# A float32 kernel of mixers, attention and FFNs: small steps of its stages rebuilt and reordered

## The chip, the core and the metric

The kernel runs on one core of a Trainium2 chip. The metric is device time in microseconds of one execution, and the time of a kernel is the median over its runs. One execution was also recorded by the hardware profiler; its rows are quoted below. TensorE is called PE, its weight loads PEld, VectorE DVE, ScalarE ACT, GpSimd POOL, and the engine that issues most of the transfers SP.

## The reference, cut to what matters

Two blocks run over 256 tokens of width 1024, all in float32. The first has two layers, each of four sublayers; the second has one layer.

```python
for l in range(2):
    h = swiglu(rms_norm(x, norm_pre[l, 0]), ffn1_gate[l], ffn1_up[l], ffn1_down[l])
    x = x + 0.5 * rms_norm(h, norm_post[l, 0])
    h = parallel_head_groups(rms_norm(x, norm_pre[l, 1]), ...)      # retention and gated delta rule
    x = x + rms_norm(h, norm_post[l, 1])
    h = memory_cross_attention(rms_norm(x, norm_pre[l, 2]), rms_norm(mem, mem_norm[l]), ...)
    ...
```

In `parallel_head_groups` the gated delta rule works on four heads, two directions and chunks of 64 tokens. It needs the decays, which are exponentials of differences of running sums of `g` within a chunk, and the solution of a unit lower triangular system per chunk:

```python
g = jnp.cumsum(g.reshape(b, h, n, c), axis=-1)
decay = jnp.exp(jnp.where(tril, g[..., :, None] - g[..., None, :], -jnp.inf))
lower = jnp.where(strict, jnp.einsum('bhnid,bhnjd->bhnij', k_beta, k) * decay, 0.0)
sol = lax.linalg.triangular_solve(lower, rhs, left_side=True, lower=True, unit_diagonal=True)
```

## The kernel before

**Tiling.** The 256 tokens are two tiles of 128 (`t` = 0, 1). Stages follow one another: `ffn1_0`, `mix_0`, `xat_0`, `ffn2_0`, the same four with `_1`, then the second block (`blk2_0`: a mixer, and a last `ffn`). Every large product is three products of split operands: `mm3` (L168) multiplies high by high, high by low and low by high part, each in one pass. A weight unit comes by SP into one of four `raw` buffers, and `unit` (L135) makes its high part on ACT (L148) and its low part on DVE (L149), in the pools `wts` (4 buffers, `self.wp`) or `w2` (8 buffers). Products that are not split run in plain float32; the trace shows each of those as two matmul records, and the transposes as one.

**Order.** The program is traced in order, and a planner sets each engine's queue: by the order of the program, except that an instruction whose operands are late in the planner's own estimate lets later ones pass. An engine then runs its queue strictly in order. `tc.issue_after(ins)` puts what a block traces on the engine of `ins` behind it.

**Stage ends.** `residual` (L286) takes a stage's sums from PSUM, norms them (`rstd`, L208: squares on ACT, then eight instructions on one column, L213 and L189 to L193, on POOL), scales them (`hg`, L296, L298) and adds them to `x` (L300). `set_pre` (L254) then prepares the next stage's input: `xg` is `x` times the gain (L235), or also times another `rstd` where the norm isn't deferred (L237). `take_pre` transposes `xg` on PE (L250) and splits it into `xT`. The end of tile 1 is kept in `self.late` and run by `run_late` inside the next stage.

**FFN** (L312). `by_tokens(t, j)` (L348) is 24 products of 512 columns for one tile and one slice `j` of the hidden width, followed by a tanh on ACT (L364) and `h` on DVE (L365, L366); `flush` transposes `h` (L371). `by_channels` does the slices from 2 on for both tiles at once. `DN(t, j)` (L408), 12 products of 512 columns, adds slice `j` to the output. The entry is L429 to L461: `by_tokens(0, 0)`, `run_late`, `by_tokens(0, 1)` with `take_pre(1)` inside it, and only later `by_tokens(1, 0)` and `(1, 1)`. At the end come `DN(0, 8)` to `DN(0, 10)`, tile 0's residual, and `DN(1, 7)` to `DN(1, 10)`. `wpool` (L329) names the pool of each unit.

**Mixer** (L724). A stream of projections (`fill`) is advanced by `more()` between the steps of the chains. `strengths` makes `g`; `decays` (L795) makes, per direction, three banks of running sums by float32 products (L805), two of them with a mask product (L807), and four exponentials from each. `inverse` (L1024) inverts the triangular blocks per direction: it copies 16 blocks into `md` (L1034, 16 ACT instructions for both directions), transposes them on DVE (L1038), and runs a long elimination on DVE (L1050, L1051). `solve` (L1117) applies the inverse to both directions by products on a quarter of PE each: direction 0 uses one half of the partitions and direction 1 the other (L1145, L1153). `rotary_tables` (L644) is called once by a hook of `ffn1_0`.

**Start.** `build` (L1786 to L1802) runs 16 products on zeros, loads tile 0 of `x`, the gain broadcast to all partitions (512 KB), two weight units, tile 1 of `x` and two more units. The identity that transposes need lies in `cst`, loaded by POOL (L84).

## Time and profile before

| | us |
|---|---|
| median of 3 runs | 1946.12 (1944.95 to 1948.43) |
| profiled execution, its time | 1947.42 |
| its span, first to last instruction | 1945.2 |
| PE busy | 1914.7 (98%) |
| DVE busy | 1412.7 (73%) |
| ACT busy | 1048.9 (54%) |
| POOL busy | 185.7 (10%) |

The span begins and ends 2.2 us inside the execution's own time. The granted clock was 0.998 of full speed over the span. Matmuls are pipelined: an interval between two starts tells what one costs PE, and its own duration is longer than that. A row in brackets names how long the engine sat idle before the instruction and what released it.

### The profile page before, as it was taken

To read this page: it belongs to the slowest core of one execution; us is meant where nothing else is said; L and a number is where in the kernel's file an instruction comes from. 1 tells how busy PE (TensorE), PEld (TensorE's weight loads), DVE (VectorE), ACT (ScalarE), POOL (GpSimd) and SP (SyncE) were. 2 spreads that over 40 slices of the span, in tenths; PEclk is the share of its full clock that TensorE was granted. 3 is DMA by queue.
4 is the path that set the end of the run, shared out by engine and by line. 5 is a ranking of instruction groups with operands and counts; after the bars stand their busy time and mean duration, and the time that the engine had idled before them with its cause. 6 is when DMAs were issued, how large, how long until landed. Compare 5 with 4: busy or idle time off the path is not lost.

```text
span 1945.2 us, 34675 instructions
## 1 busy us (share of the span) xinstructions
PE 1914.7 (98%) x12859; PEld 1717.7 (88%) x12859; DVE 1412.7 (73%) x3002; ACT 1048.9 (54%) x2173; POOL 185.7 (10%) x407
## 2 busy tenths in 40 slices
PE   9999999999999999999999999999999999999998
PEld 6899888898899989999788978998999998888997
DVE  6777688775666766667987757666798988767765
ACT  5655465465554555546555645554555555546542
POOL 2000100020200110010100120002101111001000
PEclk9999999999999999999999999999999999999999
DMA  8666434364566556644434726655566646656651
GB/s 266 206 220 217 125 109 147 109 220 137 164 205 196 180 186 220 187 161 144 137 101 145 247 86 212 200 189 157 146 174 182 187 121 205 200 196 224 199 179 49
DMA packets 272887, 337.26 MB, mean 173 GB/s; under 512 B 19740, under 2 KB 223150, under 8 KB 272718
## 3 DMA queue, kind: packets, MB, share of 16 engines
q1 hardware_dynamic: 266980, 326.64, 53.6%
q10 hardware_dynamic: 5690, 8.25, 1.2%
q8 instruction: 101, 1.65, 0.3%
q14 instruction: 68, 0.56, 0.1%
q0 software_dynamic: 48, 0.16, 0.0%
HBM read 333.90 MB, written 1.08 MB: 172 GB/s over the span
## 4 chain that ended last, share of the span: by engine, by line
PE 84%; DVE 4%; POOL 3%; DMA 2%; ACT 2%; issue 2%; SPq 0%; ACTq 0%; POOLq 0%; DVEq 0%
PE bank L170 25%; PE bank L171 25%; PE bank L172 25%; DVE lo L149 2%; DMA raw<-in_ffn_up_dram 2%; PE bank L250 1%; POOL t L192 1%; POOL vh L213 1%; POOL y L193 1%; ACT hi L148 1%; PE bank L1003 1%; PE bank L1543 1%; ACT md L1034 1%; PE bank L1153 1%; PE bank L1256 1%
## 5 line engine op out<-in xcount | busy, mean ns | idle before, releaser
L148 ACT ACTIVATE hi<-raw 128x512 fp32r<-128x512 f32 (+1 forms) x1190 | 678.7, 615 | 413.6 <-PE bank L172 96.0
L149 DVE TENSOR_TENSOR lo<-raw,hi 128x512 fp32r<-128x512 f32 (+1 forms) x1190 | 764.7, 680 | 187.1 <-ACT hi L148 178.4
L170 PE MATMUL bank<-xh,hi 128*128 128x256 f32 x2080 | 588.8, 283 | 0.0
L171 PE MATMUL bank<-xl,hi 128*128 128x256 f32 x2080 | 585.1, 281 | 0.0
L172 PE MATMUL bank<-xh,lo 128*128 128x256 f32 x2080 | 584.7, 281 | 0.1
L170 PEld LDWEIGHTS bank<-xh,hi 128*128 128x128 f32 x2080 | 394.2, 190 | 4.1
L171 PEld LDWEIGHTS bank<-xl,hi 128*128 128x128 f32 x2080 | 393.9, 189 | 3.5
L172 PEld LDWEIGHTS bank<-xh,lo 128*128 128x128 f32 x2080 | 394.5, 190 | 0.6 <-DVE lo L149 0.6
L170 PE MATMUL bank<-hi,xh 128*128 128x512 f32 (+1 forms) x852 | 333.5, 392 | 3.5 <-ACT xh L175 2.2
L171 PE MATMUL bank<-lo,xh 128*128 128x512 f32 (+1 forms) x852 | 324.7, 381 | 5.2 <-DVE lo L149 5.1
L172 PE MATMUL bank<-hi,xl 128*128 128x512 f32 (+1 forms) x852 | 323.9, 380 | 0.5 <-DVE xl L177 0.5
L171 PEld LDWEIGHTS bank<-lo,xh 128*128 128x128 f32 x852 | 160.3, 188 | 34.8 <-DVE lo L149 9.9
L170 PEld LDWEIGHTS bank<-hi,xh 128*128 128x128 f32 x852 | 160.2, 188 | 31.5 <-ACT xh L175 3.5
L172 PEld LDWEIGHTS bank<-hi,xl 128*128 128x128 f32 x852 | 159.9, 188 | 28.8 <-DVE xl L177 2.2
L170 PE MATMUL bank<-hi,hh 128*128 128x512 f32 x440 | 175.9, 400 | 1.3 <-ACT hh L175 1.3
L171 PE MATMUL bank<-lo,hh 128*128 128x512 f32 x440 | 173.9, 395 | 0.0
L172 PE MATMUL bank<-hi,hl 128*128 128x512 f32 x440 | 173.4, 394 | 0.0
L213 POOL TENSOR_SCALAR vh<-ss 128x1 f32<-128x1 f32 x40 | 27.6, 689 | 1130.8 <-ACT junk L205 996.1
L402 ACT ACTIVATE th<-s 128x256 f32<-128x256 f32 x90 | 37.3, 414 | 124.3 <-DVE s L401 122.7
L172 PEld LDWEIGHTS bank<-hi,hl 128*128 128x128 f32 x440 | 82.7, 188 | 20.7 <-DVE hl L177 0.3
L170 PEld LDWEIGHTS bank<-hi,hh 128*128 128x128 f32 x440 | 82.7, 188 | 18.4 <-ACT hh L175 1.7
L171 PEld LDWEIGHTS bank<-lo,hh 128*128 128x128 f32 x440 | 82.7, 188 | 16.0
(369 smaller groups left out, 1991.4 us busy)
## 6 DMA issues: line engine op xcount, KB each, us to landing
raw<-in_w_in_dram SPq DMA_DIRECT2D x112, 512.0 KB, 4.4
raw<-in_ffn_gate_dram SPq DMA_DIRECT2D x176, 256.0 KB, 3.9
raw<-in_ffn_up_dram SPq DMA_DIRECT2D x176, 256.0 KB, 4.3
raw<-in_ffn_down_dram SPq DMA_DIRECT2D x88, 512.0 KB, 4.6
raw<-in_w_in_dram SPq DMA_DIRECT2D x96, 192.0 KB, 2.8
raw<-in_w_ffn_gate_dram SPq DMA_DIRECT2D x44, 256.0 KB, 3.8
raw<-in_w_ffn_up_dram SPq DMA_DIRECT2D x44, 256.0 KB, 4.1
raw<-in_w_ffn_down_dram SPq DMA_DIRECT2D x22, 512.0 KB, 4.6
```

The source lines that it names most:

```text
L148: nc.scalar.activation(hi[:, c], raw[:, c], AF.Copy)
L149: nc.vector.tensor_tensor(lo[:, c], raw[:, c], hi[:, c].bitcast(F32), ALU.subtract)
L170: mm(out, lhsT=lh, rhs=rh, start=start, stop=False)
L171: mm(out, lhsT=lh, rhs=rl, start=False, stop=False)
L172: mm(out, lhsT=ll, rhs=rh, start=False, stop=stop)
L192: V.tensor_scalar(t, y, y, vh, ALU.mult, ALU.mult)
L193: V.tensor_scalar(y, t, -1.5, y, ALU.add, ALU.mult)
L213: V.tensor_scalar(vh, s[:, 0:1], s[:, 1:2], 0.5 * EPS, ALU.add, ALU.add)
L250: self.nc.tensor.transpose(b[:, i * P:(i + 1) * P], src[:, (q + i) * P:(q + i + 1) * P], self.ident)
L402: last["A"] = nc.scalar.activation(th, s[:, 0], AF.Tanh)
L1003: T.matmul(b[:, j * 256:(j + 1) * 256], lhsT=lhs[:, h, j * P:(j + 1) * P], rhs=rhs[:, h], start=True, stop=True)
L1034: A.activation(md[r, :, :, :, s], mn[r, :, :, c0:c0 + 16].rearrange("p n h a -> p a h n"), AF.Copy, scale=self.half[s][r])
```

## The change

The steps, as they stand in the diff:

- At the start, 12 products on zeros instead of 16; the gain comes as eight rows of 128 (4 KB), is transposed by PE and copied to eight columns; `x` itself is transposed, and the splits of `xT` (one per 128 columns, eight instead of two on ACT and on DVE) multiply by those columns. Tile 1 of `x` is loaded behind one weight unit instead of two.
- In the first stage alone, where `self.late` is None, `by_tokens` of both tiles take turns at every weight unit, for slice 0 and then for slice 1.
- In the other FFN entries, the second half of the late residual (the sum into `x`, `set_pre`) is traced with `issue_after` behind the tanh and `h` of `by_tokens(0, 0)`.
- The eight column instructions of `rstd` move from POOL to DVE in `residual` and in `set_pre` where the norm isn't deferred.
- `wpool` names pools by `j` and `q` instead of by a count; the `raw` buffers lie on the other side of the memory.
- `rotary_tables` handles both tiles in one set of instructions, and its sine is traced one hook later.
- `decays` takes the running sums from four float32 products for all heads, splits them into high and low parts in 36 rows, and spreads each head's sums by one-pass products with a selecting column; the mask products stay one-pass, two of 256 columns per head.
- The 16 copies into `md` move from ACT to POOL.
- In `solve` each product is issued behind the one before it, in the order head 0 direction 0, head 0 direction 1, head 1 direction 0 and so on.

```diff
-        self.rawp = pool(ctx, "raw", 4)
+        self.rawp = ctx.enter_context(tc.tile_pool(name="raw", bufs=4, side="right", reuse_waits="tile"))
...
+        self.selr = self.fp.tile([P, 4], F32R, name="selr")
...
-    def to_xT(self, src, xT, t, k0=0, nk=8, scale=1.0):
+    def to_xT(self, src, xT, t, k0=0, nk=8, scale=1.0, cols=None):
...
+            for i in range(m):
+                ix = (slice(None), k0 + q + i, slice(t * P, (t + 1) * P))
+                self.split(xT[0][ix], xT[1][ix], b[:, i * P:(i + 1) * P], cols[:, q + i:q + i + 1])
...
-        r = None if defer else self.rstd(self.halves(self.x[t]), D, pool)
-        xg = self.normed(self.x[t], g, r)
+        r = None if defer else self.rstd(self.halves(self.x[t]), D)
+        xg = self.x[t] if cols is not None else self.normed(self.x[t], g, r)
...
-            r = self.rstd(acc, D, self.nc.gpsimd)
+            r = self.rstd(acc, D)
...
-            for xh, s in zip(self.halves(self.x[t]), self.halves(hg)):
-                V.scalar_tensor_tensor(xh, s, r, xh, ALU.mult, ALU.add)
-        if gpre is not None:
-            self.set_pre(t, gpre, defer)
+        with ExitStack() as es:
+            for ins in self.behind:
+                es.enter_context(self.tc.issue_after(ins))
+            if gpost is not None:
+                for xh, s in zip(self.halves(self.x[t]), self.halves(hg)):
+                    V.scalar_tensor_tensor(xh, s, r, xh, ALU.mult, ALU.add)
+            if gpre is not None:
+                self.set_pre(t, gpre, defer)
...
-                cnt[0] += 1
-                if j == 1 or kind == "dn" and (j > 6 or j == 0):
-                    return w2
-                return self.wp if j == 10 or cnt[0] % 3 == 0 else w2
+                if kind == "dn":
+                    return self.wp if 1 < j < 8 else w2
+                return self.wp if j == 10 or j in (8, 9) and q % 2 else w2
...
+                    if k % 2:
+                        yield
...
-            by_tokens(0, 0)
-            done = [last["A"].ins, last["V"].ins]
-            self.run_late()
-            by_tokens(0, 1, {4: flush, 6: lambda: self.take_pre(1)})
+            alone = self.late is None
+            if alone:
+                one, two = by_tokens_parts(0, 0), by_tokens_parts(1, 0)
+                next(one)
+                self.take_pre(1)
+                self.fence = self.last
+                for _ in range(3):
+                    next(two)
+                    next(one)
+                next(two)
...
+                one, two = by_tokens_parts(0, 1), by_tokens_parts(1, 1)
...
+            else:
+                by_tokens(0, 0)
+                done = [last["A"].ins, last["V"].ins]
+                self.behind = done
+                self.run_late()
+                self.behind = []
+                by_tokens(0, 1, {4: flush, 6: lambda: self.take_pre(1)})
...
+            if alone:
+                flush()
+                DN(1, 0)
+            else:
+                by_tokens(1, 0)
+                flush()
+                by_tokens(1, 1)
+                flush()
...
+        V.tensor_scalar(ang, ang, 3.1415925, -3.1415925, ALU.min, ALU.max)
+        yield
+        nc.scalar.activation(cs, ang, AF.Sin)
...
+                gg = w512()[:, :144].rearrange("p (t d c) -> p t d c", t=2, d=2)
+                V.memset(gg, 0.0)
+                for c in (0, 32):
+                    V.tensor_copy(gg[:, :, :, c:c + 4], g.rearrange("p t (d c) -> p t d c", d=2))
...
+                for d in range(2):
+                    T.matmul(pg[:, 16 + d * 4:20 + d * 4], lhsT=self.ones.to_broadcast([P, P]), rhs=g[:, d, d * 4:d * 4 + 4], start=True, stop=True)
+                    for n in range(2):
+                        t = n if d == 0 else 1 - n
+                        T.matmul(b[0:36, (2 * d + n) * P:(2 * d + n + 1) * P], lhsT=gg[:, t, d], rhs=self.tri[d], start=True, stop=True)
...
+                A.copy(gr[0:36], b[0:36])
+                V.tensor_tensor(gr[32:36], b[32:36], gr[32:36].bitcast(F32), ALU.subtract)
...
-                    for h in range(4):
-                        T.matmul(b[:, h * P:(h + 1) * P], lhsT=g[:, t, d * 4 + h:d * 4 + h + 1].to_broadcast([P, P]), rhs=self.tri[d], start=h == 0, stop=h == 3 and not masked)
-                    if masked:
-                        T.matmul(hd(b), lhsT=self.identr, rhs=self.mskr[d].unsqueeze(1).to_broadcast([P, 4, P]), start=False, stop=True)
...
+                for h in hs:
...
+                    sel = self.selr[:36, h:h + 1].to_broadcast([36, P])
+                    own, far = self.bank(), self.bank()
+                    T.matmul(own, lhsT=sel, rhs=gr[:36], start=True, stop=False)
+                    T.matmul(far[:, 0:256].rearrange("p (d c) -> p d c", d=2), lhsT=sel, rhs=gr[:36].rearrange("p (d t c) -> p d t c", d=2, t=2)[:, :, 1], start=True, stop=True)
+                    for d in range(2):
+                        T.matmul(own[:, d * 256:(d + 1) * 256].rearrange("p (t c) -> p t c", t=2), lhsT=self.identr, rhs=self.mskr[d].unsqueeze(1).to_broadcast([P, 2, P]), start=False, stop=d == 1)
...
-                        A.activation(md[r, :, :, :, s], mn[r, :, :, c0:c0 + 16].rearrange("p n h a -> p a h n"), AF.Copy, scale=self.half[s][r])
+                        nc.gpsimd.tensor_scalar(md[r, :, :, :, s], mn[r, :, :, c0:c0 + 16].rearrange("p n h a -> p a h n"), self.half[s][r], None, ALU.mult)
...
+                turns = [(h, d) for h in range(4) for d in range(2)]
+                in_turn = lambda one: self.tc.issue_after(one.ins) if one else nullcontext()
...
-                        for h in range(4):
-                            for d in range(2):
-                                T.matmul(bs[d][r[d], h * P:(h + 1) * P], lhsT=Z[d][r[d], h, n], rhs=rhs[d][r[d], h], start=True, stop=True)
+                        one = None
+                        for h, d in turns:
+                            with in_turn(one):
+                                one = T.matmul(bs[d][r[d], h * P:(h + 1) * P], lhsT=Z[d][r[d], h, n], rhs=rhs[d][r[d], h], start=True, stop=True)
...
+    load_x(0)
+    g0 = net.gp.tile([P, D], F32, tag="gain", name="g0")
+    nc.sync.dma_start(g0[:8, :P], pre_of(stages[0]).rearrange("o (k p) -> (o k) p", p=P))
+    early = [units[0]()]
+    load_x(1)
+    net.stash = early + [u() for u in units[1:]]
...
-        for _ in range(16):
+        for _ in range(12):
...
-    g0 = net.bcast(net.gp, pre_of(stages[0]), D, "gain", nc.sync)
-    net.stash = [u() for u in units[:2]]
-    load_x(1)
-    net.stash += [u() for u in units[2:]]
+    nc.tensor.transpose(b[:, :8], g0[:8, :P], net.ident[:8, :8])
+    nc.scalar.copy(g0[:, P:P + 8], b[:, :8])
     for t in range(2):
-        net.set_pre(t, g0, deferred(stages[0]))
+        net.set_pre(t, None, deferred(stages[0]), g0[:, P:P + 8])
```

## Rows read from the trace of the kernel before

**Rows 1.** The page's first part: busy us and share of the span, instructions.
```profile
PE 1914.7 (98%) x12859; PEld 1717.7 (88%) x12859; DVE 1412.7 (73%) x3002; ACT 1048.9 (54%) x2173; POOL 185.7 (10%) x407
```

**Rows 2.** Waits of PE: line waited for; us in total, times, longest us.
```profile
PE bank L171 <- DVE lo L149: 5.1, 7, 1.2
PE bank L371 <- DVE h L366: 4.7, 3, 1.7
PE bank L250 <- DVE xg L237: 2.7, 3, 1.3
PE bank L170 <- ACT hh L175: 1.3, 1, 1.3
```

**Rows 3.** Timeline, first 18 us: start, us, engine, line, operation, [idle <-releaser].
```profile
1.24 0.73 POOL L84 DMA_DIRECT2D cst<-in_consts_dram  x1 [0.81 <-POOLq L1863]
6.48 0.70 DVE L235 TENSOR_TENSOR xg<-x,gain 128x512 f32<-128x512 f32 x1 [5.37 <-DMA gain<-in_norm_pre_dram]
9.39 0.50 PE L170 MATMUL bank<-hi,xh 128*128 128x512 f32 x1 [0.90 <-ACT hi L148]
17.50 0.47 ACT L364 ACTIVATE th<-bank,rh 128x256 f32<-128x256 f32 x1 [0.29 <-PE bank L172]
```

**Rows 4.** The tile `cst`: its transfer (L84), from issue to landing.
```profile
DMA to landing us min/median/max: 5.6/5.6/5.6
```

**Rows 5.** Timeline of PE, 238.2 to 239.6 us: the decays' products.
```profile
238.28 0.28 PE L172 MATMUL bank<-xh,lo 128*128 128x256 f32 x1
238.40 1.05 PE L805 MATMUL bank<-cst,g 128*128 128x128 f32 x8
239.21 0.47 PE L807 MATMUL bank<-mskr,identr 128*128 128x512 f32 x1
239.52 1.95 PE L805 MATMUL bank<-cst,g 128*128 128x128 f32 x16
```

**Rows 6.** Timeline of PE, two stretches of the solve.
```profile
332.38 1.09 PE L1153 MATMUL bank<-ch,iv 64*64 64x128 f32 x16
333.40 0.50 PE L170 MATMUL bank<-hi,xh 128*128 128x512 f32 x1
...
344.27 1.08 PE L1153 MATMUL bank<-ch,iv 64*64 64x128 f32 x8
345.29 0.49 PE L172 MATMUL bank<-hi,xl 128*128 128x512 f32 x1
```

**Rows 7.** Timeline of DVE, ACT and PE at the entry of `ffn2_0`, 494 to 499 us.
```profile
494.56 1.42 DVE L300 SCALAR_TENSOR_TENSOR x<-hg,y,x 128x512 f32<-128x512 f32 x2 [4.32 <-POOL y L193]
495.41 0.63 ACT L205 ACTIVATE junk<-x 128x512 f32<-128x512 f32 x1 [6.42 <-DVE x L300]
498.27 0.44 PE L371 MATMUL bank<-cst,h 128*128 128x128 f32 x2 [1.66 <-DVE h L366]
```

**Rows 8.** Timeline of DVE at the entry of the second block.
```profile
1357.97 1.72 DVE L237 SCALAR_TENSOR_TENSOR xg<-x,y,gain 128x512 f32<-128x512 f32 x2 [3.02 <-POOL y L193]
```

**Rows 9.** Timeline of DVE at the kernel's end: first and last of eight norm instructions.
```profile
1927.46 0.22 DVE L213 TENSOR_SCALAR vh<-ss 128x1 f32<-128x1 f32 x1
...
1929.33 0.21 DVE L193 TENSOR_SCALAR y<-t,y 128x1 f32<-128x1 f32 x1
```

**Rows 10.** Timeline of ACT and DVE, 270 to 278 us: the inverse begins.
```profile
270.70 7.58 ACT L1034 ACTIVATE md<-M,cst 32x128 f32<-32x128 f32 x16
...
276.40 0.71 DVE L1038 STREAM_TRANSPOSE w<-md 128x512 f32<-128x512 f32 x1 [3.23 <-ACT md L1034]
```

**Rows 11.** Lines of POOL by form: count, busy us, mean ns, idle before.
```profile
L192 POOL TENSOR_SCALAR t<-y,vh 128x1 f32<-128x1 f32 x120 | 50.3, 419 | 12.1
L1526 POOL TENSOR_TENSOR w<-xs,dsk 128x512 f32<-128x512 f32 x8 | 9.9, 1245 | 47.9 <-ACT w L1535 31.2 <-PE bank L1543 16.7
L634 POOL TENSOR_TENSOR w<-w,rot 128x256 f32<-128x256 f32 x8 | 6.0, 745 | 0.0
```

**Rows 12.** Timeline of POOL, 1401 us: a rotation beside DVE's splits.
```profile
1401.29 0.98 POOL L633 TENSOR_TENSOR w<-w,rot 128x192 f32<-128x192 f32 x1
```

More of the change, by code (lines that the diff above doesn't have):

```diff
@@ L1 @@
 import math
-from contextlib import ExitStack
+from contextlib import ExitStack, nullcontext
 import numpy as np
@@ L348, in by_tokens, with by_tokens_parts @@
             def by_tokens(t, j, between={}):
+                for _ in by_tokens_parts(t, j, between):
+                    pass
+            def by_tokens_parts(t, j, between={}):
                 if j not in gu:
@@ L434, in ffn @@
             xT = self.xT
-            by_tokens(0, 0)
-            done = [last["A"].ins, last["V"].ins]
-            self.run_late()
-            by_tokens(0, 1, {4: flush, 6: lambda: self.take_pre(1)})
+            alone = self.late is None
[8 more added lines that the diff above has]
+                next(two)
+                for _ in range(2):
+                    next(one, None)
+                    next(two, None)
+                done = [last["A"].ins, last["V"].ins]
+                one, two = by_tokens_parts(0, 1), by_tokens_parts(1, 1)
+                for n in range(5):
+                    next(one, None)
+                    if n == 2:
+                        flush()
+                        flush()
+                    next(two, None)
+            else:
+                by_tokens(0, 0)
+                done = [last["A"].ins, last["V"].ins]
+                self.behind = done
+                self.run_late()
+                self.behind = []
+                by_tokens(0, 1, {4: flush, 6: lambda: self.take_pre(1)})
             self.fence = done
             DN(0, 0)
-            by_tokens(1, 0)
-            flush()
-            by_tokens(1, 1)
-            flush()
+            if alone:
[3 more added lines that the diff above has]
+                by_tokens(1, 0)
+                flush()
+                by_tokens(1, 1)
+                flush()
             diag = []
@@ L456, in ffn @@
                 if j == 2:
-                    DN(1, 0)
+                    if not alone:
+                        DN(1, 0)
                 elif j < 9:
@@ new lines, in rotary_tables @@
+        wk = self.nrm.tile([P, 512], F32, tag="junk", name="wk")
+        ang, k = (wk[:, c:c + 256].rearrange("p (t c) -> p t c", t=2) for c in (0, 256))
+        pi, pf = once[:, 0:2].bitcast(I32), once[:, 2:4]
+        nc.scalar.dma_start(pi, self.a["positions"][0].rearrange("(t p) -> p t", p=P))
+        V.tensor_copy(pf, pi)
+        cs = self.fp.tile([P, 2, P], F32, name="cs1")
+        for t in range(2):
+            V.tensor_scalar(ang[:, t, 64:128], once[:, C_FREQ - C_END:C_FREQ - C_END + 64], pf[:, t:t + 1], None, ALU.mult)
@@ L679, in mem_xT @@
+        c2 = float(np.array(int(c2), np.uint32).view(np.float32))
+        c3 = 2 * math.pi - c1 - c2
+        for c in (c1, c2, c3):
+            V.scalar_tensor_tensor(ang, k, -c, ang, ALU.mult, ALU.add)
+        V.tensor_scalar(ang[:, :, 0:64], ang[:, :, 0:64], math.pi / 2, None, ALU.add)
+        V.tensor_scalar(ang, ang, 3.1415925, -3.1415925, ALU.min, ALU.max)
+        yield
+        nc.scalar.activation(cs, ang, AF.Sin)
+        self.cs1 = [cs[:, t] for t in range(2)]
     def mem_xT(self, l):
@@ L1141, in solve @@
                             bs = [self.bank() for _ in range(2)]
-                            for h in range(4):
-                                for d in range(2):
-                                    o = order[d][0]
-                                    T.matmul(bs[d][r[d], h * P:(h + 1) * P], lhsT=M[d][o, h, cols[d] + r[d].start:cols[d] + r[d].stop], rhs=y[d][o, h], start=True, stop=True)
+                            one = None
+                            for h, d in turns:
+                                o = order[d][0]
+                                with in_turn(one):
+                                    one = T.matmul(bs[d][r[d], h * P:(h + 1) * P], lhsT=M[d][o, h, cols[d] + r[d].start:cols[d] + r[d].stop], rhs=y[d][o, h], start=True, stop=True)
                             for d in range(2):
@@ L1150, in solve @@
                         bs = [self.bank() for _ in range(2)]
-                        for h in range(4):
-                            for d in range(2):
-                                T.matmul(bs[d][r[d], h * P:(h + 1) * P], lhsT=Z[d][r[d], h, n], rhs=rhs[d][r[d], h], start=True, stop=True)
+                        one = None
+                        for h, d in turns:
+                            with in_turn(one):
+                                one = T.matmul(bs[d][r[d], h * P:(h + 1) * P], lhsT=Z[d][r[d], h, n], rhs=rhs[d][r[d], h], start=True, stop=True)
                         A.copy(y[0][r[0]], hd(bs[0])[r[0]])
```

92 lines of the change are left out of this document (37 added, 55 removed).

## The prediction

> **What bounds the kernel now.** I read the page's first part first: PE is busy for 98% of the span, DVE for 73%, POOL for 10% [rows 1]. So PE's own work sets the time, and only two things shorten the kernel: work taken off PE, or a stall of PE taken away. The waits of PE come next. The list is short: four kinds that this change can reach make 13.8 us, namely low halves of weights not ready (5.1), `h` of an FFN entry not ready (4.7), `xg` of a stage entry not ready (2.7) and one late `hh` (1.3) [rows 2]. Last I read the timeline around each of these waits, to see which engine was late and what it had been queued behind. The costs below are made against the profiled execution, 1947.4 us, which is 1.3 above the median of the runs; the result is then moved down by that.
>
> **The start.** The first product leaves at 9.39, and the evacuation of tile 0's slice 0 begins at 17.50 [rows 3]. Between them stand 24 products. One of 256 columns follows its neighbour after 0.12 (238.28 to 238.40, [rows 5]), so one of 512 costs about 0.24 and 24 of them 5.8; 8.1 passed, so 2.3 went in waits for weights. The identity issued at 1.24 lands 5.6 later, at 6.84 [rows 3, 4], and no transpose can come before it, in either kernel; that is also why four zero products fewer are priced at nothing. The gain's 512 KB, for which DVE waited until 6.48 [rows 3], no longer stand ahead of the weights. Transposing the gain and the first four blocks and splitting the first column should take about 1 us from 6.84, so the first product at 7.8: 1.6 gained. Each weight unit then serves 12 products (2.9 us) instead of 6, so the waits of 2.3 mostly go; in their place comes a wait for tile 1 of `x`, its squares on ACT and its eight column splits, which I price at 1.0 (they queue ahead of the high parts on ACT). That is 1.6 + 2.3 - 1.0 = 2.9, say **3.0**; ends 1.0 (first product no earlier than identity plus the old 2.2 us, part of the waits left) and 5.0 (no new wait, and the later small waits of this entry gone too).
>
> **The decays.** Four float32 products show as eight records and take 0.81, the mask product behind them 0.31 (238.40, 239.21 and 239.52, [rows 5]). A direction has three such groups and two masks: 3 x 0.81 + 2 x 0.31 = 3.05, and two directions in two layers make 12.2. After: six float32 products more per layer at 0.20 each make 2.4 in all. Per head there is one selection of 512 columns (0.24), one of 256 (0.12) and two masks of 256 (half of 0.31 each): 0.67, times 4 heads and 2 layers 5.4. The saving is 12.2 - 7.8 = **4.4**; with masks at 0.12 and nothing for the change between the two kinds of product it is 5.2, with the short products at 0.16 and the selection at 0.31, 3.5. The exponentials stay 24 per layer. The extra small DVE and ACT steps stand in a stretch where PE has projections to do, so they cost nothing; if that cover is gone it is under 1 us a layer, within the ends.
>
> **The solve in turns.** Where both directions alternate, 16 records leave room for the next product 1.02 after they began; where one direction runs alone, 8 records need the same 1.02 [rows 6]. The two quarters of PE then work at once, or one sits idle. In layer 0 three of the six steps alternate already (near 332, 360 and 366) and three run apart (near 340, 345 and 355), and so it is in layer 1. Forcing the turns saves 1.02 for each of six: **6.0**, with ends 0 (the planner puts other products between the two of a pair) and 6.1. The added order makes direction 0 wait for direction 1; on PE the projections of `fill` can go ahead of it, so I price that wait at nothing.
>
> **Stage entries.** At the entry of `ffn2_0` DVE sat idle 4.32 for POOL's last norm step and ACT 6.42 for the sum that follows it, while the tanh of `by_tokens(0, 0)` stood behind in ACT's queue; PE then idled 1.66 for `h` [rows 7]. All three entries of this kind make the 4.7 of [rows 2]. With `issue_after` the tanh and `h` go first; what is late next is `xg` of tile 1, needed 18 products (4.3 us) after `by_tokens(0, 1)` begins. `h` takes about 1.4, the sum 1.4 and `xg` 1.3, so it is just in time: **4.0**, ends 0 and 4.7. At the other entries `xg` waits for POOL (3.02 of DVE's idle time at the second block, [rows 8]) and PE lost 2.7 [rows 2]. Eight norm instructions on DVE take from 1927.46 to 1929.54, 2.1 us [rows 9]; on POOL the three t steps alone are 1.26 [rows 11], and DVE sat idle 3.0 to 4.3 for a chain [rows 7, 8]. I take **2.4** of the 2.7, ends 0 and 2.7. The price: 16 residual chains and 10 of `set_pre` move, 26 x 2.1 = 55 us of DVE time, behind which low halves of weights queue; DVE is at 73% and PE has units in hand, so I charge **-1.0**, ends 0 and -5.0.
>
> **The inverse's copies.** ACT's 16 copies take 7.58, 0.474 each, and hold back the high parts of weights; DVE idles 3.23 for them [rows 10], and in each layer PE then waits 1.2 for a low half, half of the 5.1 of [rows 2]. On POOL nothing else is queued, but no row shows such a copy there. Below it lies the one-column step (0.42), above it the two-operand step of 256 columns (0.745) [rows 11]; 128 columns of one operand are nearer the first, so about 0.5, the same total as on ACT. Then only the relief of ACT is left: **2.4** gained. Ends: at 0.42 some 4 gained; at 0.745, 16 x (0.745 - 0.474) = 4.3 per layer lost less 1.2, so -6.2 in all. What queues behind the transposes of DVE then is the low halves, and PE waits for those. [...] No row here shows a strided POOL read.
>
> **The rest.** The late `hh` (1.3, [rows 2]) stands behind the sine's table load and its wait for DVE; the sine moved by a hook no longer waits for DVE but still loads its table: **0.6**, ends 0 and 1.3. In `wpool` the units of `dn` 7 now sit in the four `wts` buffers until `DN(1, 7)`, while all four units of slice 10 want those buffers; the planner must draw `DN(0, 8)`, `DN(0, 9)` and `DN(1, 7)` ahead of part of `by_channels(0, 10)`. PE's work is the same, but less of it is left to cover tile 0's residual (12 products or 2.9 us per `DN`): **-2.5**, ends 0 and -7.
>
> **Sum.** 3.0 + 4.4 + 6.0 + 4.0 + 2.4 - 1.0 + 2.4 + 0.6 - 2.5 = 19.3. The profiled execution would be 1928.1, the median 1946.1 - 19.3 = **1926.8**. All good ends together give some 29, all bad ones some -14.
>
> **Rivals.** *Only PE's work counts.* The stalls come back elsewhere, since the planner misjudged POOL and may misjudge DVE (the 6.42 of [rows 7] is such a misjudgement), and the solve pairs in part: 3.0 + 4.4 + 3.0 = 10.4, so 1936. For it: stalls are short and each has a next one close behind. Against: the waits named have one clear late engine.
> *The buffers of `dn` 7 cost every FFN.* Five FFNs each expose 4 us of the residual; then 20 instead of 2.5 is lost and the time is 1926.8 - 2.5 + 20 = 1944, no change. Against it: after `ffn1` and the last FFN the residual isn't PE's next need.
> *POOL is the bound of the inverse (slower).* If a copy costs what POOL takes for 512 columns, 1.245 [rows 11], because POOL and DVE hold each other up, the 16 copies take 19.9 instead of 7.58 in each layer, DVE's transposes and the elimination behind them come 12.3 later, and the projections in hand run out: 1926.8 + 2.4 + 2 x 12.3 = 1954. It decides from (1946.1 - 1926.8 - 2.4) / 32 + 0.474 = 1.0 us a copy. For it: beside DVE's splits a POOL step of 192 columns took 0.98 [rows 12], more than one of 256 took on average (0.745). Against: 512 columns with two operands are far from 128 with one. [...]
>
> **How the numbers follow.** The forecast has 0.62 (its own range 1915 to 1935), only PE's work 0.19 (1930 to 1941), better than all of it 0.05 (under 1914), the buffers 0.07 (1940 to 1948), POOL as the bound 0.07 (1947 to 1960). The range from 1914 to 1941 leaves out the last three and a little more, under 2 in 10. A measurement of this kernel can tell about 0.2%, 3.9 us, from no change. Faster by more than that means under 1942.2: 0.62 + 0.19 + 0.05 and a sixth of the buffers' 0.07, 0.87; within it 0.06; slower 0.07.
>
> **What would show it.** In the profile after, the decays' float32 group should be gone and one selection should take about 0.24; every group of L1145 and L1153 should show 16 records; PE's waits for `h` and `xg` should be near nothing; the first product should start near 7.8; a POOL copy should take 0.4 to 0.75 and DVE's wait for it should stay under 4. A POOL copy over 1.0, PE waits for low halves over 10 us, or stalls at the entries after `ffn2` would make the prediction wrong.

## The result and the profile after

The changed kernel takes 1990.9 us (median of 4 runs, 1987.7 to 1993.6) against 1945.8 before: 1.0229 times as long, 95% interval 1.0216 to 1.0242. The forecast was 1926.8, faster. The profiled execution took 1990.73, its span is 1989.0, and the granted clock over the span is 0.984 where it was 0.998.

The page's first part of the changed kernel, which answers to [rows 1], and in a second fence the waits of PE, which answer to [rows 2] (line waited for; us in total, times, longest):

```profile
PE 1927.8 (97%) x12808; PEld 1729.3 (87%) x12808; DVE 1454.9 (73%) x3215; ACT 1034.0 (52%) x2154; POOL 132.2 (7%) x231
```
```profile
PE bank L174 <- DVE lo L152: 17.2, 4, 8.1
PE bank L254 <- DVE xg L240: 11.5, 8, 2.5
PE bank L824 <- DVE w L815: 9.1, 2, 4.6
PE bank L1140 <- issue: 4.8, 2, 2.5
PE bank L869 <- DVE gr L829: 3.0, 2, 1.6
```

PE is still the busy engine, but it now has few long waits in place of many short ones. The waits for `h` and `hh` of [rows 2] are gone. Low halves went from 5.1 to 17.2 and `xg` from 2.7 to 11.5, and there are three new kinds, at the decays (L824 `gg`, here named by its pool `w`, and L869 `gr`) and in a run of small products of the inverse (L1140).

The windows of PE around the two longest stops (us of the window, busy us, instructions, granted clock, DMA share, GB/s):

```profile
244.00:246.00 2.00, 0.00 (x0) 0.77 0.80 262
246.00:250.00 4.00, 2.00 (x9) 0.50 0.38 118
250.00:254.00 4.00, 4.00 (x13) 0.50 0.00 0
...
288.00:292.00 4.00, 0.40 (x3) 1.00 0.00 0
292.00:294.00 2.00, 0.00 (x0) 0.72 0.00 0
...
297.00:299.00 2.00, 2.00 (x6) 0.50 0.41 80
```

After each stop PE works on for some us at a granted clock of 0.50. Products of 256 columns then start every 0.21 (253.08 to 253.29) instead of 0.12 (255.74 to 255.86), those of 512 every 0.43 (297.50 to 297.93) instead of 0.23 (300.59 to 300.82). A stop of 5 to 8 us thus costs more than its own length.

Both kernels have the same 10392 large products (`mm3`). So the start of the n-th of them can be compared: its lag is that start minus the start in the kernel before, in us. The last two columns are runs that are described below: e5 undoes two parts of the change, e12 holds the parts that are worth keeping.

| n-th large product | place | changed | old decays, md on ACT (e5) | kept parts (e12) |
|---|---|---|---|---|
| 240 | first stage | -0.9 | -1.3 | -1.8 |
| 1080 | end of `ffn1_0` begins | -3.1 | -3.5 | -4.3 |
| 1320 | `mix_0` begins | 3.0 | 1.9 | -3.8 |
| 1680 | after its inverse | 21.8 | 1.8 | -3.9 |
| 1920 | after its solve | 19.8 | -0.2 | -5.9 |
| 2640 | in `ffn2_0` | 19.0 | -1.1 | -6.9 |
| 5040 | in `mix_1` | 21.4 | 1.1 | -9.5 |
| 5520 | after its solve | 41.3 | -1.3 | -11.5 |
| 6240 | in `ffn2_1` | 37.7 | -2.9 | -12.7 |
| 7440 | in the second block | 44.2 | 2.6 | -13.2 |
| 10320 | end | 43.8 | 2.7 | -13.6 |

Each mixer loses 17 to 20, each passage from a stage to the next up to 6.5.

### The profile page after: what moved, and what is told of

It is laid out like the page before. It is cut to its first block, busy times and chain, and to the rows that moved or that the text cites. A ratio compares the mean times of both kernels' runs of the same rounds, so it can differ in the third digit from the quotient of the medians.

```text
span 1989.0 us, 34510 instructions
## 1 busy us (share of the span) xinstructions
PE 1927.8 (97%) x12808; PEld 1729.3 (87%) x12808; DVE 1454.9 (73%) x3215; ACT 1034.0 (52%) x2154; POOL 132.2 (7%) x231
## 4 chain that ended last, share of the span: by engine, by line
PE 85%; DVE 6%; DMA 3%; ACT 2%; issue 1%; POOL 1%; SPq 0%; ACTq 0%; DVEq 0%
PE bank L173 25%; PE bank L174 25%; PE bank L175 25%; DVE lo L152 2%; PE bank L254 1%; POOL md L1095 1%; ACT hi L151 1%; DMA raw<-in_ffn_up_dram 1%; DMA raw<-in_ffn_down_dram 1%; ACT junk L208 1%; PE bank L1298 1%; PE bank L1321 1%; PE bank L1608 1%; PE bank L1232 1%; PE bank L1218 0%
## 5 line engine op out<-in xcount | busy, mean ns | idle before, releaser
L174 PEld LDWEIGHTS bank<-xl,hi 128*128 128x128 f32 x2080 | 398.3, 192 | 3.3
L174 PE MATMUL bank<-lo,xh 128*128 128x512 f32 (+1 forms) x852 | 326.2, 383 | 17.2 <-DVE lo L152 17.2
L174 PEld LDWEIGHTS bank<-lo,xh 128*128 128x128 f32 x852 | 162.2, 190 | 43.8 <-DVE lo L152 18.7
L418 DVE TENSOR_TENSOR s<-bank,rows 128x512 f32<-128x512 f32 x90 | 61.8, 687 | 90.3 <-PE bank L175 65.3
```

Of the source, the lines that this page charges most:

```text
L174: mm(out, lhsT=lh, rhs=rl, start=False, stop=False)
L418: nc.vector.tensor_tensor(s, bb, rows[0], ALU.mult)
```

## The experiments

Ratios are to the kernel before on the same chip, with 95% intervals; a difference of two ratios is uncertain by some 2 to 5 us.

| run | kernel | median us | ratio |
|---|---|---|---|
| e1 | changed, md copies on ACT | 1978.7 | 1.0153 (1.0136 to 1.0171) |
| e2 | changed, `gg` in its own buffer | 1988.8 | 1.0209 (1.0190 to 1.0228) |
| e3 | both | 1974.8 | 1.0136 (1.0119 to 1.0153) |
| e4 | e3, norm chains on POOL | 1975.5 | 1.0146 (1.0125 to 1.0167) |
| e5 | md on ACT, old decays | 1949.6 | 1.0013 (1.0005 to 1.0022) |
| e6 | e3, hooks moved | 1958.5 | 1.0061 (1.0046 to 1.0076) |
| e7 | before, md copies on POOL | 1961.1 | 1.0071 (1.0058 to 1.0084) |
| e8 | e2, copies in another order | 1990.1 | 1.0218 (1.0200 to 1.0236) |
| e9 | e5, no forced turns | 1955.5 | 1.0033 (1.0021 to 1.0045) |
| e10 | e5, norm chains on POOL | 1950.6 | 1.0010 (1.0001 to 1.0018) |
| e11 | e5, old pools and raw buffers | 1935.4 | 0.9933 (0.9922 to 0.9945) |
| e12 | e11, norm chains on POOL | 1933.5 | 0.9926 (0.9914 to 0.9939) |
| e13 | e5, old raw buffers | 1948.3 | 1.0009 (0.9999 to 1.0018) |
| e14 | e5, old rule for pools | 1933.9 | 0.9938 (0.9924 to 0.9953) |
| e15 | e12 and the new decays, hooks moved | 1945.4 | 0.9995 (0.9986 to 1.0004) |
| e16 | e15, selections of 128 rows | 1937.6 | 0.9946 (0.9932 to 0.9960) |

### The copies into md: e1, e7, e8

e1 undoes this part alone, and e7 does it alone on the kernel before:

```diff
-nc.gpsimd.tensor_scalar(md[r, :, :, :, s], mn[r, :, :, c0:c0 + 16].rearrange("p n h a -> p a h n"), self.half[s][r], None, ALU.mult)
+A.activation(md[r, :, :, :, s], mn[r, :, :, c0:c0 + 16].rearrange("p n h a -> p a h n"), AF.Copy, scale=self.half[s][r])
```

> The changed kernel with one part undone: the 16 copies into md stand on ACT again. The changed kernel's time is 1990.9. Theory A (the copies on POOL cost 0.82 each in a row instead of 0.47, the low halves of weights stand behind DVE's transposes of md, PE stops for 8.3 twice and then runs at the lower clock for some 5 us): the stretch that lost 8.4 in each layer comes back, so 1972 to 1975, and PE's wait for low halves falls from 17 to under 4. Rival B (the projections are used up by this point because of the earlier stop in the decays, so PE waits here whoever copies): PE still waits over 4 for the inverse in each layer and the time stays above 1982.

> The kernel before with one part of the change alone: the 16 copies into md on POOL. Theory A (the copies cost 0.82 in a row, DVE's transposes of md wait for them and the low halves behind DVE's transposes): as in the changed kernel, 7 per layer lost, 1958 to 1964. Rival B (the forecast's sum by the copy's measured price alone: 16 x (0.82 - 0.47) = 5.6 per layer less 1.2 of relief): 1953 to 1956. Rival C (projections in hand hide it, the stop in the changed kernel came from work used up earlier): under 1949.

e1 came to 1978.7, 12 below the changed kernel and 4 above the expected 1972 to 1975, and PE's waits for low halves fell to 6.0, not under 4; with `gg` in a buffer of its own (e2 against e3) the same edit is worth 14.0. e7 came to 1961.1, as theory A had it; its lag rises by 7.2 in layer 0 and by 7.9 in layer 1, all of it at the inverse. Rival C falls: even in the kernel before, with no other loss ahead of it, the projections in hand don't hide the copies.

The timeline of the changed kernel at the inverse, POOL, DVE and PE, which answers to [rows 10], and from e7 the waits of PE for low halves:

```profile
281.37 13.07 POOL L1095 TENSOR_SCALAR md<-M,cst 32x128 f32<-32x128 f32 x16 [0.71 <-DVE M L1059]
288.28 0.71 DVE L1099 STREAM_TRANSPOSE w<-md 128x512 f32<-128x512 f32 x1 [4.57 <-POOL md L1095]
294.48 0.71 DVE L1099 STREAM_TRANSPOSE w<-md 128x512 f32<-128x512 f32 x1 [5.49 <-POOL md L1095]
296.49 0.80 PE L174 MATMUL bank<-lo,xh 128*128 128x512 f32 x1 [8.09 <-DVE lo L152]
```
```profile
PE bank L171 <- DVE lo L149: 16.9, 7, 7.7
```

Sixteen copies take 13.07, 0.82 each, where ACT's took 7.58. DVE is idle for 4.57 and again for 5.49. The low halves stand behind its transposes, so PE waits through both. The order of DVE's queue has a part in this. In the kernel before, a low half is made between the two transposes of layer 0, as its timeline shows:

```profile
277.04 0.65 DVE L149 TENSOR_TENSOR lo<-raw,hi 128x512 fp32r<-128x512 f32 x1
...
278.31 0.71 DVE L1038 STREAM_TRANSPOSE w<-md 128x512 f32<-128x512 f32 x1 [0.29 <-ACT md L1034]
```

In e7 the second transpose comes at 282.24 and the next low half at 283.51, behind both, although its high part is done. PE's stop there grows from 1.2 to 7.7. How much of this is the price of the copies and how much the order, no run separates.

e8 turns the order of elements round, so that the read has neighbouring elements in a row:

```diff
-nc.gpsimd.tensor_scalar(md[r, :, :, :, s], mn[r, :, :, c0:c0 + 16].rearrange("p n h a -> p a h n"), ...)
+nc.gpsimd.tensor_scalar(md[r, :, :, :, s].rearrange("p a h n -> p n h a"), mn[r, :, :, c0:c0 + 16], ...)
```

> The changed kernel with gg in its own buffer (1988.8) and POOL's copies into md in another order of elements: they read 16 neighbouring elements in a row instead of one in every 128 or more, and write with the wide step instead. If the wide step of the read is the price, a copy falls from 0.72 (DVE idle) to 0.5 or less and the time by 5 or more. If it is POOL's price for an instruction of this size, whatever the order, a copy stays at 0.68 to 0.75.

The line of the copies in e8 (duration ns, minimum, median, maximum):

```profile
L1095 POOL TENSOR_SCALAR md<-M,cst x32: 699/715/748, 280.6 to 977.1; 32x128 f32<-32x128 f32 x32
```

In the changed kernel the median is 720 and the maximum 1314; its line, and a row of DVE's timeline there:

```profile
L1095 POOL TENSOR_SCALAR md<-M,cst x32: 705/720/1314, 281.4 to 978.6; 32x128 f32<-32x128 f32 x32
283.04 0.67 DVE L152 TENSOR_TENSOR lo<-raw,hi 128x512 fp32r<-128x512 f32 x1
```

The step of the read alone isn't the price: between the two reads the medians differ by 5 ns in 720. POOL takes 0.7 for this size of instruction, while DVE waits and does nothing. One copy in each layer took 1.31 (at 282.92 and 967.83), while DVE makes a low half (at 283.04 and 967.96); the other copies took 0.70 to 0.75, and in e7 the longest took 1.33. That POOL and DVE hold each other up there is not shown: in e8 DVE makes a low half during the copies too (282.31), and none is longer than 0.75. The write has the wide step in e8, so that a price of steps as such isn't excluded.

### The decays: e2, e3, e5, e6

```diff
-gg = w512()[:, :144].rearrange("p (t d c) -> p t d c", t=2, d=2)
+gg = bp.tile([P, 144], F32, tag="gg", name="gg").rearrange("p (t d c) -> p t d c", t=2, d=2)
```

> The changed kernel with one edit: the tile gg of the decays gets a buffer of its own instead of one of the six w512 buffers that the convolutions use. Theory A (the zeroing of gg waited for a buffer that a convolution gives back, then stood in DVE's queue behind ten of its steps; PE stopped 4.6 and 1.4 in each layer and ran at half clock for some 9 us after it): PE's wait for gg disappears, 9 to 10.5 per layer come back, 1970 to 1973. Rival B (DVE is simply full there; with its own buffer gg is a little earlier and PE waits nearly as long, for the sums' low parts or for the exponentials): a wait of over 2 in each layer remains at the decays and the time stays above 1981.

> The changed kernel with both edits: gg in a buffer of its own, the copies into md on ACT. If the two stops are separate losses, their gains add: 1952 to 1957, with the granted clock back near 1.0. If they share a cause (work in hand that one stop leaves to the other), the sum is short by 5 or more: above 1960. Either way it stays above the kernel before (1945.8) if the norm chains on DVE and the stop in the 32-column products are losses of their own.

The changed kernel's timeline at the decays, PE and DVE, which answers to [rows 5], and below it the same place in e2 (ACT, DVE, PE):

```profile
246.61 1.89 PE L824 MATMUL bank<-cst,w 128*36 128x128 f32 x8 [4.58 <-DVE w L815]
249.89 0.79 PE L869 MATMUL bank<-gr,selr 36*128 36x512 f32 x1 [1.39 <-DVE gr L829]
...
244.51 1.51 DVE L664 SCALAR_TENSOR_TENSOR acc<-bank,cw,acc 128x255 f32<-128x255 f32 x3
...
246.22 0.25 DVE L815 COPY w<-g 128x16 f32<-128x16 f32 x2
```
```profile
238.40 0.63 PE L824 MATMUL bank<-cst,gg 128*36 128x128 f32 x4
...
245.88 0.63 ACT L665 ACTIVATE th<-acc 128x512 f32<-128x512 f32 x1 [2.36 <-DVE acc L664]
246.41 0.56 ACT L828 CAST gr<-bank 36x512 fp32r<-36x512 f32 x1
...
247.26 0.68 DVE L829 TENSOR_TENSOR gr<-bank,gr 4x512 fp32r<-4x512 f32 x1
...
248.00 0.79 PE L869 MATMUL bank<-gr,selr 36*128 36x512 f32 x1 [5.92 <-DVE gr L829]
```

Rival B of e2 was right: only 2 came back (3.9 by the ratios, which their intervals don't tell from nothing). `gg` is now copied at 232.5 instead of 246.2 and the sums are done at 239.0, but PE stops as long as before, for `gr`. Its copy on ACT stands behind a tanh that waits for DVE's taps, the subtraction on DVE stands behind the same taps, and the selections come 9.0 after the sums. The buffer was the first link of this way round, not its cause. So e3 got the 14 of the copies and hardly more, and came out 18 above the expected 1952 to 1957.

e5 puts the decays of the kernel before back (L805 and L807 of the old code), with md on ACT:

> The changed kernel with the decays of the kernel before and the copies into md on ACT; the rest of the change stays. With gg in its own buffer PE waited as long as before, now for gr: its sums go from PE to ACT (behind a tanh that waits for DVE's taps), to DVE (behind the taps) and back to PE, 9.2 from sums to use, and PE's order leaves 24 products (2.9) between them. Theory A (this way round is the cost, 6.1 of stop and some 4.5 of lower clock in each layer): compared with the run with both edits (1974.8) about 10 per layer come back, 1952 to 1957. Rival B (the projections run out there in any case, because the other parts of the change use work up earlier): a stop of over 3 in each layer remains at the decays, time above 1964.

1949.6, below the expected range: 25.2 less than e3. The stop at the decays is gone, and so is the one at L1140. So the new decays, with the stop at L1140 counted in, cost 12 to 14 in a layer, the largest part of the loss.

e6 keeps them and hangs their steps at other projections:

```diff
-values(0, ...), *qkv(1, {0: s}), *qkv(2, {0: s, 1: s, 3: s}),
+values(0, ...), *qkv(1, {0: s, 3: s}), *qkv(2, {2: s, 3: s}),
```

> The run with both edits (gg in its own buffer, md on ACT, 1974.8), and the steps of strengths hung at other projections: the sums one step earlier, the first decays one step later, so that 96 products (11.5) instead of 24 stand between the sums and the first selection. Theory A (only the way round PE, ACT, DVE, PE was uncovered): no wait for gr, the saving of the new decays (2.2 per layer) is kept, 1947 to 1953. Rival B (the eight selections and 24 exponentials now stand in one piece and hold ACT and PE's banks up later, before the inverse): a new stop of 3 or more between the decays and the inverse, above 1958.

1958.5, on the edge of rival B: the wait for `gr` falls to 0.6 in each layer, but PE stops 2.6 at the inverse instead of 1.2 in e5, and the decays still cost 9 against e5.

### The decays again: e15 and e16

e15 puts the new decays, with `gg` and hooks as in e6, into the kernel of e12 (below).

> The kernel of the kept parts (1933.5) and the new decays, with gg in its own buffer and 96 products between the sums and the first selection. Theory A (the saving of PE's work that was forecast, 2.2 per layer, is real once the way round is covered): 1928 to 1931. Rival B (the selections and exponentials in one piece push the inverse later, which cost some 4 in a layer in the run with moved hooks): 1936 to 1942.

1945.4, 12 more than e12 and worse than either expectation, though the way round is covered. Timeline of PE in e15, and in a second fence its windows:

```profile
243.66 0.47 PE L871 MATMUL bank<-gr,selr 36*128 36x512 f32 x1 [0.60 <-DVE gr L831]
243.98 0.27 PE L872 MATMUL bank<-gr,selr 36*128 36x256 f32 x1
244.18 0.51 PE L874 MATMUL bank<-mskr,identr 128*128 128x256 f32 x2
244.62 0.50 PE L871 MATMUL bank<-gr,selr 36*128 36x512 f32 x1
```
```profile
245.00:247.00 2.00, 2.00 (x9) 0.93 0.06 24
247.00:249.00 2.00, 2.00 (x5) 0.50 0.00 0
249.00:251.00 2.00, 2.00 (x6) 0.50 0.03 8
```

A head takes 0.96 here, at the full clock; the forecast had 0.67. And the clock falls to 0.50 for some 7 us, while PE is busy in every window from 245 on.

e16 multiplies by 128 rows, 92 of them zero:

```diff
+nc.gpsimd.memset(gr.bitcast(F32), 0.0)
-sel = self.selr[:36, h:h + 1].to_broadcast([36, P])
-T.matmul(own, lhsT=sel, rhs=gr[:36], start=True, stop=False)
+sel = self.selr[:, h:h + 1].to_broadcast([P, P])
+T.matmul(own, lhsT=sel, rhs=gr, start=True, stop=False)
```

> The kernel of the kept parts with the new decays (1945.4), and the selections multiply 128 rows, 92 of them zero, instead of 36: the same products, columns and order. Theory A (products that use 36 of 128 rows bring the granted clock down to 0.5, as at 246.9 in that run): the clock stays at 1.0 through the decays, 3 to 3.5 per layer come back, 1937 to 1940. Rival B (the stop of 0.6 for gr, or the mixture of short products, brings it down): the clock falls as before and the time stays within 2 of 1945.4.

The same two views in e16:

```profile
244.14 0.40 PE L872 MATMUL bank<-gr,selr 128*128 128x512 f32 x1
244.37 0.28 PE L873 MATMUL bank<-gr,selr 128*128 128x256 f32 x1
244.49 0.40 PE L875 MATMUL bank<-mskr,identr 128*128 128x256 f32 x2
244.72 0.40 PE L872 MATMUL bank<-gr,selr 128*128 128x512 f32 x1
```
```profile
246.00:248.00 2.00, 2.00 (x10) 1.00 0.41 86
```

1937.6, as theory A had it, and the clock stays at 1.00. A head now takes 0.58. But two more things moved with the rows: the wait of 0.6 is gone, and the planner issued the heads in two groups instead of one. So the shorter products are shown; that the rows alone keep the clock up is not.

With these products the lag against e12 falls by 2.2 from product 1320 to 1500 in layer 0, and by 2.2 from 4980 to 5160 in layer 1, which is what was forecast per layer. It is given back at the inverse, where PE stops 2.7 and 2.6 instead of 1.2. In layer 0 the copies into md begin only 0.3 earlier than in e12 (266.58 against 266.88), and the low half that DVE makes between its two transposes in e12 (273.25) is made behind both in e16 (275.42). No run tests which of these makes the longer stop. In whole mixers e16 loses 0.5 and 0.2 against e12; the rest of the 4 between them lies outside the mixers, and no run shows why.

### Norm chains: e4 and e10

```diff
-r = self.rstd(acc, D)
+r = self.rstd(acc, D, self.nc.gpsimd)
```

and likewise in `set_pre` where the norm isn't deferred.

> As the run with both edits, and the 26 norm chains of residual and set_pre on POOL again. In the changed kernel such a chain takes 2.1 only where DVE has nothing else; interleaved with splits it takes 4 to 7. Theory A (the move to DVE is no gain, and the late chains are what PE waits for at the entries of the memory attention and of the second block): 3 to 8 faster than the run with both edits. Rival B (a POOL chain, 3.0 at best, is the later one, as I forecast): 2 to 5 slower than it.

> Same base (1949.6), the 26 norm chains of residual and set_pre on POOL again. Theory A (a chain takes 3.9 on average on DVE between splits and took 3.8 on POOL: no gain either way): within 2 of 1949.6. Rival B (the waits of PE for xg, 10.8 in the base and 2.7 before the change, come from DVE's chains): 1941 to 1945.

1975.5 against 1974.8, and 1950.6 against 1949.6: no difference that can be told. From the first of the eight instructions to the end of the last, the 26 chains that moved take 3.9 each on average in the changed kernel and took 3.8 on POOL. The timeline of DVE shows why ([rows 9] is the undisturbed one): between the first and the last step of the chain that begins at 428.07 other work is queued, and 2.1 become 5.8.

```profile
428.07 0.20 DVE L216 TENSOR_SCALAR vh<-ss 128x1 f32<-128x1 f32 x1
...
429.35 1.40 DVE L240 SCALAR_TENSOR_TENSOR xg<-x,y,gain 128x512 f32<-128x512 f32 x2
...
433.67 0.20 DVE L196 TENSOR_SCALAR y<-t,y 128x1 f32<-128x1 f32 x1
```

### Pools: e11, e13, e14

e11 undoes the rule of `wpool` and the side of the `raw` buffers, e13 the buffers alone, e14 the rule alone:

```diff
-if kind == "dn":
-    return self.wp if 1 < j < 8 else w2
-return self.wp if j == 10 or j in (8, 9) and q % 2 else w2
+cnt[0] += 1
+if j == 1 or kind == "dn" and (j > 6 or j == 0):
+    return w2
+return self.wp if j == 10 or cnt[0] % 3 == 0 else w2
```

> Same base (1949.6), the old rule for the pools of weight units and the raw buffers on the old side. Theory A (the new rule moves the end of the FFN and with it the memory's transposes, where PE loses 3.5 between 176 and 191 and 1 to 2 at the other FFN ends): 1943 to 1947. Rival B (those waits come from the memory's norm chain on POOL and not from the pools): within 1.5 of 1949.6.

> The changed kernel with the old decays and the md copies on ACT (1949.6), the raw buffers alone as before; the new rule for pools stays. Theory A (the rule is the cost: the units of dn sit in the pool that the next units want, so the next stage's units are loaded late): within 3 of 1949.6. Rival B (the raw buffers' new side and reuse delay the loads): 1935 to 1939.

> Same base (1949.6), the old rule for pools alone; the raw buffers stay on the new side. Theory A (the rule is the cost): 1934 to 1938, and at the end of ffn2_0 no load is issued later than some 12 after the first down product. Rival B (the raw buffers): within 3 of 1949.6.

e11 gains 14 (over twice what was expected at best), e14 as much, e13 nothing. So it is the rule. At the end of `ffn2_0` the down products begin at 678.60 in the changed kernel. Timeline there, SP, ACT, DVE and PE:

```profile
694.99 0.47 SPq L146 DMA_DIRECT2D raw<-in_ffn_up_dram  x1
...
691.69 3.24 ACT L151 ACTIVATE hi<-raw 128x512 fp32r<-128x512 f32 x6 [2.08 <-DMA raw<-in_ffn_up_dram]
...
692.36 0.69 DVE L152 TENSOR_TENSOR lo<-raw,hi 128x512 fp32r<-128x512 f32 x1 [1.32 <-ACT hi L151]
...
696.63 0.63 PE L254 MATMUL bank<-cst,xg 128*128 128x128 f32 x4 [1.31 <-DVE xg L238]
```

The last gate and up units of the next stage are issued at 694.99, 16.4 after the first down product; in e14 at 656.92, 3.2 after it (653.68). So ACT waits for a unit that lands late, DVE waits for ACT in the middle of tile 0's norm chain, and `xg` comes late. The loads are late at all five ends of FFNs: in e5, by the same product, 5 to 11 fewer have been issued than in e14, and the lag of e5 against e14 rises there by 5.0, 3.5, 0.8, 4.7 and 1.2. The norm chain on DVE isn't what makes this dear: e10 and e12 both have it on POOL, and with the new rule e10 is 17 slower than e12, whose rule is the old one (their raw buffers differ too, which e13 shows to be worth nothing). At this place in e10 the chain is done undisturbed, the units are late, and PE waits 0.6 for an `xh` behind ACT.

### The turns: e9

```diff
-in_turn = lambda one: self.tc.issue_after(one.ins) if one else nullcontext()
+in_turn = lambda one: nullcontext()
```

> Base: the changed kernel with the old decays and the md copies on ACT (1949.6), the last run's kernel of that kind. One part more undone: the products of the solve are issued freely again, without the forced turns. Theory A (the turns pair what ran apart, as forecast, though the stretch of the solve shows only 2.0 per layer gained): 4 slower, 1953 to 1955. Rival B (the planner pairs them by itself now): within 1 of 1949.6.

1955.5, 5.9 more in us and 0.20% more (3.9) by the ratios: the turns are worth about 4. The timeline of PE in the changed kernel, which answers to [rows 6]:

```profile
360.52 0.43 PE L1209 MATMUL bank<-ch,M 64*64 64x128 f32 x2
363.64 1.08 PE L1209 MATMUL bank<-ch,M 64*64 64x128 f32 x14
```

Direction 0's first product goes alone, as nothing binds it, and the other seven come later in turns.

### The parts that are worth keeping: e12

e12 has the new start, the sine's hook, the late residual behind `h` and the turns; decays, md copies, norm chains and pools are those of the kernel before.

> The kernel before with the parts that the traces show as gains: the new start and the sine one hook later, the second half of the late residual behind h, the turns of the solve; old decays, md copies on ACT, norm chains on POOL, old pools. By the stretches: start 1.3, the late hh 1.5 to 2, entries of ffn2 2.0 each, solve 2.0 per layer, 11 in all: 1934 to 1940. Rival: with the old norm chains and pools the gains at the entries of ffn2 go, or new waits stand at the other entries: 1941 to 1946.

1933.5, 0.9926 of the kernel before: faster than both kernels, by 14 and by 57. Its waits of PE, which answer to [rows 2], hold neither `h` nor `hh`:

```profile
PE bank L173 <- ACT xh L178: 5.6, 6, 2.1
PE bank L174 <- DVE lo L152: 4.2, 4, 1.2
```

## Why the prediction was wrong

By the ratios (1.0229, 1.0209, 1.0136, 1.0013, 0.9938, each times 1946) the loss of 44.6 is made, in the order in which the parts were undone, of 3.9 for `gg`'s buffer, 14.2 for the md copies, 23.9 for the rest of the decays, 14.6 for the rule of the pools, less 12.1 for everything else.

| term | forecast | measured |
|---|---|---|
| decays | +4.4 | -27.8 |
| md copies | +2.4 | -14.2 |
| pools | -2.5 | -14.6 |
| start, turns, entries, norm chains, sine | +15.0 | +12.1 |

**The decays** failed at one sentence: that the extra small steps on DVE and ACT stand where PE has projections to do, so they cost nothing, "under 1 us a layer" without that cover. I named neither what is queued ahead of them (DVE's taps, ACT's tanh behind the taps) nor how many products PE's order leaves between the sums and the selections (24, or 2.9 us, for a way of 9.0). The old decays went from PE to ACT, with one small step on DVE, and not back; the new ones go from PE to ACT to DVE and back to PE. The price of the products was wrong too: 0.96 a head, not 0.67 (e15). And two costs were not thought of. One is the clock after the stop. The other is the stop at L1140: between products 1560 and 1680, and between 5280 and 5400, where it lies, the lag of e3 rises by 3.3 and 4.3 and that of e5 doesn't rise, so some 7.6 of the 23.9 stand there and not on this way round. The claim that PE's own work falls by 2.2 per layer held only in e16, and there the inverse took it back.

**The copies.** A copy took 0.72, just under my dear end of 0.745, and in the row of sixteen 0.82, above it, so the mechanism's first half was right: not the free end but the dear one. What failed is what follows from it. I had the loss at 3.1 a layer at that price, and let the rival decide from 1.0 a copy. PE lost 7.2 to 7.9 a layer in e7: the copying grew by 5.5 and the stop by 6.5, the low half between the transposes moved behind both, the relief of 1.2 never came (low halves wait on DVE, not on ACT), and the clock fell behind the stop (0.994 over the span of e7, 0.998 before). The rival's own reason, POOL and DVE holding each other up, is seen at most in the one copy of 1.31, 0.6 a layer: most copies took 0.7 while DVE was idle.

**The pools** were the second rival in all but its mechanism: it had 20 for five ends of FFNs and a chance of 0.07, the forecast had 2.5. What the runs show differs from both: not fewer products over the residual, but the next stage's units loaded late (13 later at the end of `ffn2_0`), whether the norm chain stands on DVE or on POOL.

**The start** gained 0.9 in the changed kernel and 1.3 to 1.8 in e5 and e12, instead of 3.0. In the changed kernel the first product leaves at 9.99 ([rows 3]: 9.39), not 7.8. The timeline of ACT shows that two high parts and a square are queued ahead of the first column:

```profile
7.92 1.15 ACT L151 ACTIVATE hi<-raw 128x512 fp32r<-128x512 f32 x2 [1.19 <-DMA raw<-in_ffn_up_dram]
8.98 0.61 ACT L208 ACTIVATE junk<-x 128x512 f32<-128x512 f32 x1
9.59 0.35 ACT L178 ACTIVATE xh<-bank,g 128x128 fp32r<-128x128 f32 x1
```

**The turns** gained 4 instead of 6; three steps per layer ran apart as read, and the pairs that form now are of 2 and 14.

**Stage entries.** The waits for `h` are gone, as forecast; in e12 the three entries give 5.8 (4.0 forecast, end 4.7). The norm chains gave nothing where +2.4 and -1.0 stood: the 2.1 of [rows 9] is a chain on an idle DVE, and I used it for chains between splits. **The sine**: the wait for `hh` is gone in e12 (1.7 of lag between products 240 and 480), not in e11.

The likeliest case was wrong because three parts with an unknown price were all taken near their cheap ends; each is a new wait on an engine's queue that I did not read row by row.

## What to carry to other kernels

A small step that goes from PE over other engines back to PE costs what stands in those queues: count the products between its ends and compare them with the way round (2.9 against 9.0 here), and don't price a moved chain by its duration on an idle engine (2.1 there, 3.9 on average between splits). When a step moves to a slower engine (0.82 a copy instead of 0.47), read what stands behind it in the next engine's queue, since what could go ahead may be queued behind. A change of buffers can be a change of when the next stage's loads are issued (16.4 after the first down product instead of 3.2). Work saved on PE ahead of a wait for another engine can be given back at that wait, as the 2.2 a layer of e16 were.

## What was not expected of the hardware

- Products of 36 rows among products of 128 took longer than the same products over 128 rows: 0.32 against 0.23 for 512 columns (e15 and e16), and the mask products beside them 0.22 against 0.12. The loads of the weights took as long: in the changed kernel, at the full clock, 0.18 with 36 rows and 0.19 with 128. What differs is when they start. Where the row count changes, the load starts together with its product (259.90, 260.44 and 260.87); where it stays the same, ahead of it (260.01 for the product at 260.24, 259.57 for the one at 259.69).
- In e15 the clock fell to 0.50 while PE was busy in every window; before it fell PE had stood 0.6 and then run the selections of 36 rows and their masks for 3 us. It fell in layer 1 of e15 too, to 0.73 and 0.59 on average in the windows of 5 us from 910 and 915, and in e16 it stays at 1.00 in both places.
- In the changed kernel PE stopped inside a run of 128 small products, at the 124th and, in layer 1, at the 126th:

```profile
331.62 1.28 PE L1140 MATMUL bank<-zd,f 32*32 32x32 f32 x124
335.21 0.25 PE L1140 MATMUL bank<-zd,f 32*32 32x32 f32 x4 [2.32 <-issue]
```

The trace has a transfer of 16 KB of instructions that starts at 332.95, as the products end, and one at 1018.16 in layer 1; PE goes on 2.3 after each. In e5, e11 and e12 there is no such stop, and it is shorter in e6 (1.3 at most) and in e15 (one of 0.9). That PE waits for its instructions here is the likely reason; no run was made to show it.
